# Drawing the order of a weight tile's products and the places of its blocks, tile pair by tile pair

## The chip, the core and the metric

The kernel runs on one core of one Trainium2 chip. The metric is the time of one execution on the device in microseconds (us), taken as the median over runs; smaller is better. A profile is the record of one such execution: each instruction of each engine with its start and its length.

## The reference

Two layers of an encoder over 272 rows (256 tokens and 16 learned rows), model width 2048. In each layer, cut to what matters here:

```
proj = h @ w_in                                # 2048 -> 6176 columns
y    = concat(gated linear attention, neighbourhood attention)
h    = LN(ALPHA * h + y @ w_out)               # 2048 -> 2048
h    = LN(ALPHA * h + relu(h @ w_ff1)**2 @ w_ff2)   # 2048 -> 8192 -> 2048
```

Nearly all arithmetic is in the products with `w_in`, `w_out`, `w_ff1` and `w_ff2`, in float32. After the second layer only the 256 tokens are kept, so much of that layer is computed for 256 columns and not for 272.

## The kernel before, in words

**Two halves for one float32.** TensorE is fed float32r operands. Each weight tile and each activation tile is therefore split into a high part (a rounded copy) and a low part (what the rounding left). A product is the sum of three: weight high by activation high (`h`), weight high by activation low (`l`) and weight low by activation high (`w`).

**A weight tile.** Weights come from HBM in tiles `raw` of 128 partitions by 1024 columns (512 KB), which hold eight blocks of 128 by 128. `made` (L179) takes one tile of the stream, has SP issue its DMA, and `halves` (L208) lets ScalarE copy it to `wh` (L211) and then VectorE subtract `wh` from `raw` into `wl` (L212). There are three buffers of each (`wst`, bufs=3), and `weights` (L173) keeps two tiles made ahead of the one in use. ScalarE can write a `wh` buffer only when the last product that reads it is done, and VectorE a `wl` buffer likewise; the next DMA into a `raw` buffer waits for that subtraction. The engines take their instructions in order.

**Where the blocks lie.** `blocks` makes of a flat tile a triple (access, step, pair): block j starts at `first + j // 2 * pair + j % 2 * step` elements. Before the change `wh` is packed (0, P, 2P): each block starts at a multiple of 512 bytes. For `wl` the constant LOWS gives the places: (16, P+32, 2P+64) where the tile is used in the form called once, and (0, P+48, 2P+64) otherwise. Taken within 256 bytes, the even and the odd low blocks start 64 and 192 bytes in (once), or 0 and 192 bytes in. The activations: the high half starts at a multiple of 256 bytes and the low half at 128 bytes past one (PITCH 288), or directly behind 256 high columns where the pair is dense.

**The products of one tile.** `eight` (L232 to L246) issues all products of a tile in the order of the constant TURNS, with one weight load (PEld) per product (PE):

- not once: "hlhlwwhlhlwwhlhlwwhlhlww", 24 products of 256 to 274 columns each.
- once (second layer, 256 columns, 292 tiles): "hhhhhhhhwwwwwwww". Here the high and low activations stand side by side, and an `h` is one product of 512 columns (high and low activation at once); a `w` has 256. 16 products for a tile.

Four tiles at the end of the last product are loaded for once and used in the other form (`slim`). `by_k` (L256 to L273) uses the weight blocks in an order of its own, with one product per (block, output), and not TURNS. `by_m` calls `eight` for one output block at a time and then lets other work, held in generators, issue some instructions (`pump`): attention, normalisation, evictions.

**What sets the order around the change.** The stream of tiles (`order`) is fixed, tile t+2 is made when tile t is taken, and everything on TensorE is issued in program order.

Of the kernel before, what the change touches and what calls it, by code (L numbers as in the profile page):

```python
# [8 lines left out]
F32R = mybir.dt.float32r  # L9
# [5 lines left out]
P = 128  # L15
# [11 lines left out]
WB = 1024  # L27
# [10 lines left out]
MEET = 2  # L38
PAD = 40
PITCH = 288  # L40
WIDE = 1280
LOWS = {True: (16, P + 32, 2 * P + 64), False: (0, P + 48, 2 * P + 64)}
TURNS = {True: "hhhhhhhhwwwwwwww", False: "hlhlwwhlhlwwhlhlwwhlhlww"}


class Pair(tuple):
# [10 lines left out]
class Trunk:  # L57
    def __init__(self, ctx, tc, ins, out):
        self.ctx, self.tc, self.nc = ctx, tc, tc.nc
        self.i, self.out = ins, out  # L60
        self.bg, self.fg, self.credit, self.fcredit = deque(), deque(), 0, 0
        self.wants, self.due, self.late = {}, None, 0
        self.x = [None] * DC
        self.stream, self.ready = self.order(), deque()
        pool = lambda name, **k: ctx.enter_context(tc.tile_pool(name=name, **k))
        self.cp = pool("const", bufs=1)
        self.xp = pool("xhl", bufs=1)
        self.yp = pool("yhl", bufs=1)
        self.wp = pool("wst", bufs=3)
        self.jp = pool("jn", bufs=1)  # L70
        self.pm = pool("pm", bufs=4, space=PSUM)
        self.pb = pool("pb", bufs=4, space=PSUM)
# [101 lines left out]
    def weights(self):  # L174

        while len(self.ready) < 2:
            self.ready.append(self.made(*next(self.stream, (None, (), False))))
        return self.ready.popleft()

    def made(self, ap, ends, once):  # L180
        if ap is None:
            return None
        nc = self.nc
        raw = self.wp.tile([P, WB], F32, name="raw", tag="raw")
        wh, wl = self.wp.tile([P, WB], F32R, name="wh", tag="wh"), self.wp.tile([P, WIDE], F32R, name="wl", tag="wl")
        wh, wl = self.blocks(wh, 0, P, 2 * P), self.blocks(wl, *LOWS[once])
        for c in map(slice, (0,) + ends, ends):
            nc.sync.dma_start(raw[:, c], ap[:, c])
            self.halves(raw[:, c], wh, wl, slice(c.start // P, c.stop // P))
        if not ends:  # L190
            self.head(ap, raw, wh, wl)
        return wh, wl

    def blocks(self, flat, first, step, pair):

        ap = lambda at, n: bass.AP(flat.tensor, flat.offset + first + at, [flat.ap[0]] + n + [[1, P]])
        return ap, step, pair
# [16 lines left out]
    def head(self, ap, raw, wh, wl):  # L214

        nc, q = self.nc, WB // 4
        both = self.xr.tile([P, 2, q + L], F32, name="head", tag="head", bufs=1)
        self.x[:2] = [self.pair(self.xp, "x", c) for c in range(2)]
        for c in range(2):
            nc.sync.dma_start(both[:, c], self.i["head"][:, c])  # L220
        nc.sync.dma_start(raw[:, 2 * q:], ap[:, 2 * q:])
        for c in range(2):
            at = slice(2 * c, 2 * c + 2)
            h, lo = (t[:, :L] for t in self.x[c])
            acts = lambda: self.split(both[:, c, q:], h, lo)
            weights = lambda: self.halves(both[:, c, :q], wh, wl, at)
            for f in (weights, acts) if c else (acts, weights):
                f()
        for at in (slice(4, 6), slice(6, 8)):
            self.halves(raw[:, at.start * P:at.stop * P], wh, wl, at)  # L230

    def eight(self, ps, wh, wl, x, n, first, last, once):  # L232

        mm = self.nc.tensor.matmul
        seen = dict.fromkeys("hlw", 0)
        for i, kind in enumerate(TURNS[once]):
            j = seen[kind]  # L240
            seen[kind] += 1
            w, v, o = wl if kind == "w" else wh, x[j], ps[:, :n]
            rhs = v[kind == "l"][:, :n]
            if once:
                rhs, o = (v.once, ps) if kind == "h" else (v[0][:, :T], ps[:, T:])
            mm(o, lhsT=self.block(w, j), rhs=rhs, start=first and not i, stop=last and i == len(TURNS[once]) - 1)  # L246

    def whole(self, parts):

# [956 lines left out]
```

## Time and profile before

| | |
|---|---|
| median of 2 runs | 2359.82 us (2359.66 to 2359.98) |
| the profiled execution | 2360.16 us, its span 2358.4 us |
| granted TensorE clock | 0.999 |
| PE, weight loads, VectorE, ScalarE busy | 2348.3, 2234.0, 1523.6, 1213.4 us |
| DMA | 419.02 MB, mean 178 GB/s |
| chain that ended last | PE 97% of the span |

How to read it: PE is the stream of matrix products and PEld that of the weight loads, which run beside them. A row of the groups names line, engine, operation, output tile and input tiles, sizes and count, then the busy time and the mean length of one instruction in ns. Products overlap at their ends, so the length of one is more than its distance to the next one; the distance is read from the starts in the timeline. 16096 of the 18180 products use weight tiles.

### The profile page before, as it was taken

The page shows a single profiled execution, that of the slowest core. Times are in us where ns is not written, and L with a number is a line of the kernel's source. Part 1 is how long each engine was busy: PE and PEld are TensorE (multiplying, and loading weights), DVE is VectorE, ACT ScalarE, POOL GpSimd, SP SyncE. Part 2 cuts the span into 40 slices and gives each one's busy share as a digit, 9 for nine tenths or more (in the row PEclk, how much of TensorE's full clock was granted, in tenths as well). Part 3 has the DMA queues.
Part 4 walks back from the last instruction along what each step waited for, and adds up shares of the span by engine and source line. Part 5 has one row for each costly group of instructions (what it writes and reads, how often), then busy time and mean ns, then how long its engine had stood idle before and what let it go on. Part 6 is the DMA issues. An engine that isn't in the chain of part 4 may idle for free.

```text
span 2358.4 us, 44599 instructions
## 1 busy us (share of the span) xinstructions
PE 2348.3 (100%) x18180; PEld 2234.0 (95%) x18180; DVE 1523.6 (65%) x2432; ACT 1213.4 (51%) x2100; POOL 131.4 (6%) x200
## 2 busy tenths in 40 slices
PE   9999999999999999999999999999999999999998
PEld 9999999999999999999999999999988888888888
DVE  5588777775544455546567787778866545666655
ACT  5666664564433344444457666655654333444443
POOL 0021110110000000000020111100100000000000
PEclk9999999999999999999999999999999999999999
DMA  8454445555555555555555555456566666666664
GB/s 260 153 160 153 151 141 171 170 178 179 176 174 177 177 174 178 178 175 176 177 184 160 174 167 154 156 159 199 182 194 191 193 189 194 189 192 211 202 192 146
DMA packets 118301, 419.02 MB, mean 178 GB/s; under 512 B 13512, under 2 KB 14024, under 8 KB 118096
## 3 DMA queue, kind: packets, MB, share of 16 engines
q1 hardware_dynamic: 117808, 415.65, 56.4%
q8 instruction: 142, 2.33, 0.4%
q10 hardware_dynamic: 288, 0.52, 0.1%
q14 instruction: 63, 0.52, 0.1%
HBM read 414.03 MB, written 2.10 MB: 176 GB/s over the span
## 4 chain that ended last, share of the span: by engine, by line
PE 97%; DVE 2%; issue 1%; ACT 1%; POOL 0%; DVEq 0%; ACTq 0%; POOLq 0%
PE mm L246 85%; PE mm L272 6%; PE bg L272 1%; PE bg L783 1%; PE mm L722 1%; PE bg L583 0%; DVE wl L212 0%; PE bg L429 0%; PE mm L748 0%; DVE acc L1011 0%; ACT wh L211 0%; PE mm L472 0%; PE bg L909 0%; PE bg L634 0%; PE bg L664 0%
## 5 line engine op out<-in xcount | busy, mean ns | idle before, releaser
L212 DVE TENSOR_TENSOR wl<-raw,wh 128x1024 fp32r<-128x1024 f32 (+1 forms) x770 | 942.6, 1225 | 649.1 <-ACT wh L211 644.6
L211 ACT CAST wh<-raw 128x1024 fp32r<-128x1024 f32 (+1 forms) x770 | 805.1, 1047 | 926.8 <-PE mm L246 579.5
L246 PE MATMUL mm<-x,wh 128*128 128x272 f32 (+3 forms) x5376 | 990.5, 311 | 0.0
L246 PEld LDWEIGHTS mm<-x,wh 128*128 128x128 f32 x5376 | 798.4, 188 | 38.6 <-PE mm L722 0.6
L246 PE MATMUL mm<-x,wl 128*128 128x272 f32 (+3 forms) x3264 | 590.1, 284 | 0.0
L246 PEld LDWEIGHTS mm<-x,wl 128*128 128x128 f32 x3264 | 485.4, 188 | 11.4
L246 PE MATMUL mm<-y,wh 128*128 128x272 f32 (+2 forms) x2128 | 411.4, 322 | 0.0
L246 PEld LDWEIGHTS mm<-y,wh 128*128 128x128 f32 x2128 | 325.4, 188 | 22.0
L246 PE MATMUL mm<-u,wh 128*128 128x272 f32 (+2 forms) x1552 | 299.1, 321 | 0.0
L246 PEld LDWEIGHTS mm<-u,wh 128*128 128x128 f32 x1552 | 237.1, 188 | 16.0
L246 PE MATMUL mm<-y,wl 128*128 128x272 f32 (+1 forms) x1408 | 240.5, 282 | 0.0
L246 PEld LDWEIGHTS mm<-y,wl 128*128 128x128 f32 x1408 | 204.3, 188 | 6.4
L246 PE MATMUL mm<-u,wl 128*128 128x272 f32 (+1 forms) x1024 | 175.2, 282 | 0.0
L246 PEld LDWEIGHTS mm<-u,wl 128*128 128x128 f32 x1024 | 148.8, 188 | 4.7
L272 PE MATMUL mm<-x,wh 128*128 128x272 f32 (+1 forms) x512 | 73.5, 289 | 0.0
L272 PEld LDWEIGHTS mm<-x,wh 128*128 128x128 f32 x512 | 67.9, 191 | 0.0
L999 POOL TENSOR_SCALAR acc<-acc,vec 128x272 f32<-128x272 f32 (+1 forms) x24 | 41.9, 1751 | 273.9 <-DVE acc L1011 154.2
L871 DVE TENSOR_TENSOR acc<-acc,mm 128x256 f32<-128x256 f32 (+1 forms) x71 | 30.1, 424 | 38.9 <-PE mm L246 38.9
L560 ACT COPY U<-S 128x272 f32<-128x272 f32 (+1 forms) x104 | 41.0, 429 | 19.3 <-DVE S L569 18.3
L569 DVE TENSOR_TENSOR S<-S,dec 128x272 f32<-128x272 f32 (+1 forms) x112 | 46.1, 441 | 3.7 <-ACT U L560 3.1
L294 ACT CAST u<-ft 128x272 fp32r<-128x272 f32 (+1 forms) x64 | 26.1, 408 | 41.7 <-DVE ft L827 41.7
L571 POOL TENSOR_TENSOR dec<-dec 128x272 f32<-128x272 f32 (+6 forms) x56 | 29.9, 534 | 245.9 <-DVE S L569 245.9
(265 smaller groups left out, 1634.4 us busy)
## 6 DMA issues: line engine op xcount, KB each, us to landing
raw<-in_wff SPq DMA_DIRECT2D x512, 512.0 KB, 3.6
raw<-in_win SPq DMA_DIRECT2D x190, 512.0 KB, 3.9
raw<-in_wout SPq DMA_DIRECT2D x64, 512.0 KB, 3.6
nb<-in_nab SPq DMA_DIRECT2D x16, 352.0 KB, 4.1
xraw<-in_xT SPq DMA_DIRECT2D x7, 272.0 KB, 5.5
out<-out SPq DMA_DIRECT2D x5, 256.0 KB, 3.2
brow<-in_norm SPq DMA_DIRECT2D x4, 256.0 KB, 4.9
gw<-in_wup SPq DMA_DIRECT2D x4, 196.0 KB
```

The costliest lines, as they stand in the source:

```text
L211: self.nc.scalar.copy(h, r)
L212: self.wl = self.nc.vector.tensor_tensor(lo, r, h.bitcast(F32), ALU.subtract).ins
L246: mm(o, lhsT=self.block(w, j), rhs=rhs, start=first and not i, stop=last and i == len(TURNS[once]) - 1)
L272: self.nc.tensor.matmul(ps[g + m][:, :n], lhsT=self.block(parts[p][0], 4 * j + m), rhs=acts[k + j][parts[p][1]][:, :n], start=k + j + p == ...
L294: self.nc.scalar.copy(hi, src)
L560: nc.scalar.copy(U[:, lv % 4, j, :w].rearrange("p (n t h) -> p n t h", t=2, h=hb), bass.AP(S.tensor, S.offset + 2 * j * L, [S.ap[0], [2 * ...
L569: tt(o, o, totals(lv, odd, w), ALU.mult)
L571: nc.gpsimd.tensor_tensor(d[1], d[1], d[0], ALU.mult)
L722: nc.tensor.matmul(ps[hh][:, t * NKEY:t * NKEY + NKEY], lhsT=q[hs, NM + t * P:NM + t * P + P], rhs=k[hs, t, :], start=True, stop=True)
L783: nc.tensor.matmul(po[t][hs, :P], lhsT=v2[ts, hs] if rest else v1[:, t, hs], rhs=p2[ts, hh, :] if rest else p1[:, 2 * hh + t, :], start=re ...
L871: tt(a, a, part, ALU.add)
L999: nc.gpsimd.tensor_scalar(a, a, gain, bias, ALU.mult, ALU.add)
```

## The change

Four things change in the code.

- `wh` gets the size of `wl`, and both are 1344 elements wide (before 1024 and 1280).
- For each tile, `draw` takes a number r from a multiplicative hash of `tiles // 2`, so that two tiles in a row share it. For once it leaves `wh` packed, starts the low blocks 0 to 224 bytes in, in steps of 32 bytes, and puts the odd low block another 0 to 224 bytes on. Otherwise the odd high block, the low tile's start and the odd low block each get 0, 64, 128 or 192 bytes.
- r also picks one of two orders: "hwhw..." or "hhww..." for once, and the former "hlhlww..." or "hllhww..." otherwise.
- A queue `turns` carries the order from the making of a tile to its use; `eight` reads `self.turn`, and falls back to the former order where a tile made for once is used in the other form.

```diff
-WIDE = 1280
-LOWS = {True: (16, P + 32, 2 * P + 64), False: (0, P + 48, 2 * P + 64)}
-TURNS = {True: "hhhhhhhhwwwwwwww", False: "hlhlwwhlhlwwhlhlwwhlhlww"}
+WIDE = 1344
+TURNS = {True: ("hwhwhwhwhwhwhwhw", "hhwwhhwwhhwwhhww"), False: ("hlhlwwhlhlwwhlhlwwhlhlww", "hllhwwhllhwwhllhwwhllhww")}
...
+        self.turn = self.turns.popleft()
         return self.ready.popleft()
...
-        wh, wl = self.wp.tile([P, WB], F32R, name="wh", tag="wh"), self.wp.tile([P, WIDE], F32R, name="wl", tag="wl")
-        wh, wl = self.blocks(wh, 0, P, 2 * P), self.blocks(wl, *LOWS[once])
+        high, low, turn = self.draw(once)
+        wh, wl = self.wp.tile([P, WIDE], F32R, name="wh", tag="wh"), self.wp.tile([P, WIDE], F32R, name="wl", tag="wl")
+        wh, wl = self.blocks(wh, *high), self.blocks(wl, *low)
...
+        self.turns.append(turn)
         return wh, wl
+
+    def draw(self, once):
+
+        r = self.tiles // 2 * 2654435761 % 2 ** 32 >> 8
+        self.tiles += 1
+        if once:
+            return (0, P, 2 * P), (r % 8 * 8, P + r // 8 % 8 * 8, 2 * P + 64), TURNS[once][r // 64 % 2]
+        high, low, base = (r // k % 4 * 16 for k in (1, 4, 16))
+        return (0, P + high, 2 * P + 64), (base, P + low, 2 * P + 64), TURNS[once][r // 64 % 2]
...
-        for i, kind in enumerate(TURNS[once]):
+        turn = self.turn if once or "l" in self.turn else TURNS[False][0]
+        for i, kind in enumerate(turn):
...
-            mm(o, lhsT=self.block(w, j), rhs=rhs, start=first and not i, stop=last and i == len(TURNS[once]) - 1)
+            mm(o, lhsT=self.block(w, j), rhs=rhs, start=first and not i, stop=last and i == len(turn) - 1)
```

More of the change, by code (lines that the diff above doesn't have):

```diff
@@ L63, in __init__ @@
         self.x = [None] * DC
-        self.stream, self.ready = self.order(), deque()
+        self.stream, self.ready, self.tiles, self.turns = self.order(), deque(), 0, deque()
         pool = lambda name, **k: ctx.enter_context(tc.tile_pool(name=name, **k))
@@ L181, in made @@
         if ap is None:
+            self.turns.append(None)
             return None
```

## The prediction

> **What bounds the kernel now.** I read the page first, its busy times and its chain of work.
>
> ```profile
> span 2358.4 us, 44599 instructions
> PE 2348.3 (100%) x18180; PEld 2234.0 (95%) x18180; DVE 1523.6 (65%) x2432; ACT 1213.4 (51%) x2100; POOL 131.4 (6%) x200
> PE 97%; DVE 2%; issue 1%; ACT 1%; POOL 0%; DVEq 0%; ACTq 0%; POOLq 0%
> ```
>
> TensorE never stops: 2348.3 of 2358.4 us. The profiled execution took 2360.16 us, 1.8 us around its span, and stands 0.34 us over the median of 2359.82. So the change matters by two things only: the distance from one weight product to the next, and products that would have to wait for a weight tile. Waits of this kind hardly exist now; the list of waits has one:
>
> ```profile
> PE mm L272 <- DVE wl L212: 0.6, 1, 0.6
> ```
>
> Then the timeline, two tiles of the once form and a stretch of the other form (start, length in us, engine, line).
>
> ```profile
> 2000.33 2.00 PE L246 MATMUL mm<-x,wh 128*128 128x512 f32 x8
> 2002.17 1.08 PE L246 MATMUL mm<-x,wl 128*128 128x256 f32 x8
> 2003.09 2.00 PE L246 MATMUL mm<-x,wh 128*128 128x512 f32 x8
> 2004.93 1.08 PE L246 MATMUL mm<-x,wl 128*128 128x256 f32 x8
> ...
> 699.75 0.41 PE L246 MATMUL mm<-y,wl 128*128 128x272 f32 x2
> ...
> 700.50 0.41 PE L246 MATMUL mm<-y,wl 128*128 128x272 f32 x2
> ```
>
> Take starts, not lengths. Eight `h` of 512 columns take 2004.93 - 2003.09 = 1.84 us, 230 ns each; eight `w` of 256 take 2003.09 - 2002.17 = 0.92, 115 each; a tile 2003.09 - 2000.33 = 2.76. In the other form six products take 0.75 us, 125 ns each, 3.0 us for a tile. Of the groups by shape I now take the mean length (the first number after the comma):
>
> ```profile
> L246 PE MATMUL mm<-x,wh 128*128 128x272 f32 x3584 | 595.4, 288 | 0.0
> L246 PE MATMUL mm<-x,wl 128*128 128x272 f32 x1792 | 367.5, 286 | 0.0
> L246 PE MATMUL mm<-x,wh 128*128 128x512 f32 x1152 | 289.8, 394 | 0.0
> L246 PE MATMUL mm<-x,wl 128*128 128x256 f32 x1152 | 156.6, 278 | 0.0
> L246 PE MATMUL mm<-x,wh 128*128 128x274 f32 x384 | 63.9, 289 | 0.0
> L246 PE MATMUL mm<-x,wl 128*128 128x274 f32 x192 | 40.1, 291 | 0.0
> L246 PE MATMUL mm<-x,wh 128*128 128x258 f32 x256 | 41.5, 285 | 0.0
> L246 PE MATMUL mm<-x,wl 128*128 128x258 f32 x128 | 25.9, 284 | 0.0
> L246 PE MATMUL mm<-u,wh 128*128 128x256 f32 x32 | 5.1, 282 | 0.0
> L272 PE MATMUL mm<-x,wh 128*128 128x256 f32 x128 | 17.6, 283 | 0.0
> L272 PE MATMUL mm<-x,wl 128*128 128x256 f32 x64 | 9.8, 281 | 0.0
> ```
>
> 394 - 230 = 164, 278 - 115 = 163, 288 - 125 = 163: the length is the distance and a constant 163 ns. So a difference of lengths is a difference of distances, and the lengths show what the places do. At 256 columns, packed blocks (all 0 within 256 bytes) have 282 and 283; blocks at 0 and 192 have 281; the `w` of once, at 64 and 192, have 278. That is 4 to 5 ns for not starting where the activation starts. At 272 columns the low blocks (half at 0, half at 192) are only 2 ns shorter than the packed high ones, at 258 one ns, and at 274 they are 2 ns longer.
>
> **The change, part by part.** Counts first. The once form has 292 tiles (2336 products of 512, as many of 256, 4672 in all). The other form has (14752 - 4672) / 24 = 420 tiles, and the by-k form 56.
>
> *High blocks outside once.* Two thirds of 11424 products read a high block, half of them an odd one, 3808; by the formula of the draw 356 of 472 such tiles leave place 0, so some 2871 products start elsewhere. The price for one: the low rows are half off place 0, so the difference of low to high, doubled, is -4 ns (272), -2 (258), -4 (256, by k) and +4 (274). Ends -4 and +4, -11.5 and +11.5 us. I take -1.5, because three of four rows are negative, but the row of 288 mixes products by the high and the low activation, of which the latter (at 128 bytes) never shared a place with a packed block: -4.3 us.
>
> *Low blocks outside once.* Half of 3808 products start at 0 now, a quarter after it: some 936 leave. By the same prices -3.7 to +3.7, taken -1.4 us.
>
> *Low blocks of once.* These stand well now (278). Drawn in steps of 32 bytes, an eighth of 2336 lands on 0 and pays 282 - 277.5 = 4.5 ns: 292 x 4.5 = 1.3 us. If the steps to either side pay the same, it is 35% by the draw, 3.7 us. If other places are better by 1 ns, -2.3. I take +2.5. The high blocks of once stay packed.
>
> A rule that speaks against all three: the Trainium skill, "SBUF — State Buffer", section "Who interferes with whom", gives TensorE two independent read ports, one for the moving operand and one for weight loads, and says that it never waits on anyone. By it these three terms would be 0. The rows of 278 and 282 at one width speak against it as far as TensorE's two reads of itself go.
>
> *The order in once.* What does a change between `h` and `w` cost? Rows for single products of the tile at 2003.09, in this order: the first `h`, then last `h` and first `w` together, then the last three `w`.
>
> ```profile
> L246 PE MATMUL mm<-x,wh 128*128 128x512 f32 x1 | 0.4, 395 | 0.0
> ...
> L246 PE MATMUL mm<-x,wh 128*128 128x512 f32 x1 | 0.4, 389 | 0.0
> L246 PE MATMUL mm<-x,wl 128*128 128x256 f32 x1 | 0.3, 279 | 0.0
> ...
> L246 PE MATMUL mm<-x,wl 128*128 128x256 f32 x3 | 0.5, 276 | 0.0
> ...
> L246 PE MATMUL mm<-x,wh 128*128 128x512 f32 x9 | 2.4, 393 | 0.0
> L246 PE MATMUL mm<-x,wl 128*128 128x256 f32 x10 | 1.5, 277 | 0.0
> ```
>
> An `h` before a `w` is 4 ns shorter than the mean (389 against 393); an `h` behind a `w` is 2 longer and a `w` behind an `h` is 2 longer. "hwhw" has 7 more changes of each sort, "hhww" 3 more; the draw gives 142 and 154 tiles (4 of the 296 are used in the other form). The first sort alone: 142 x -28 ns and 150 x -12 ns, -5.8 us; the other two alone +5.8. After the change each `h` in "hwhw" is of both sorts, so they cancel: 0. The new order "hllhww" outside once changes neither counts nor the last use of a buffer: 0, and any effect lies within the ends above.
>
> *The buffers.* In "hwhw" the last `h` is the last but one product, so ScalarE may overwrite `wh` some 0.8 us later (0.92 less one `w`), and `wl` is needed 230 ns into the tile, not 1.84 us.
>
> ```profile
> 1999.62 1.05 ACT L211 CAST wh<-raw 128x1024 fp32r<-128x1024 f32 x1 [1.44 <-PE mm L246]
> ...
> 2000.58 0.40 ACT L294 CAST y<-ft 128x256 fp32r<-128x256 f32 x1
> 2000.70 1.23 DVE L212 TENSOR_TENSOR wl<-raw,wh 128x1024 fp32r<-128x1024 f32 x1 [0.74 <-ACT wh L211]
> ...
> 2005.84 0.40 PE L246 MATMUL mm<-x,wh 128*128 128x512 f32 x1
> ```
>
> The cast starts when the tile before 2000.33 has done its `h`, so it fills that tile's buffer for the tile that starts at 2005.84. After the change the subtraction would end at 2001.93 + 0.8 = 2002.7 and be needed at 2006.07: 3.3 us are left. What queues behind the waiting cast on ScalarE (a copy of 0.40 us) and on SP (the next `raw`, issued when the subtraction is done) shifts by the same 0.8 us and keeps that slack. The cast's output in blocks: the subtraction already writes such blocks in 1.23 us, and 1.05 + 1.23 on two engines lies beside 2.76 of products; 0. The one thin place is after 1583, where DMAs arrive late:
>
> ```profile
> 1593.88 1.22 DVE L212 TENSOR_TENSOR wl<-raw,wh 128x1024 fp32r<-128x1024 f32 x1
> ...
> 1594.59 2.00 PE L246 MATMUL mm<-y,wh 128*128 128x512 f32 x8
> 1596.43 1.08 PE L246 MATMUL mm<-y,wl 128*128 128x256 f32 x8
> ```
>
> The subtraction ends at 1595.10; `w` starts at 1596.43 and would start at 1594.82, 0.28 us too early. Once TensorE is that much later the tiles behind it fit: +0.5 us, at most 2, at least 0.
>
> Sum: -4.3 - 1.4 + 2.5 + 0 + 0.5 = -2.7. Against its own 2360.16 this gives 2357.5, and 0.34 less for the median: **2357 us**. All low ends: -11.5 - 3.7 - 2.3 - 5.8 = -23.3, 2336.5; all high ends: 11.5 + 3.7 + 3.7 + 5.8 + 2 = 26.7, 2386.5.
>
> **The rivals.**
>
> *Places do nothing* (20%): then only the 0.5 us is left, 2360. For it: 286 and 288 are near. Against it: 278 and 282.
>
> *Places are good everywhere* (10%): 5 ns, as at 256 columns, for the 3807 products that leave place 0, -19, and -5.8 for the order: 2335.
>
> *Places are worse than the chosen ones* (14%): the row of 291 (274 columns) is then the rule, and 3807 x 4 ns + 3.7 + 5.8 + 2 make about +26: 2385.
>
> *A weight load lies open at each change from `w` to `h`* (5%), on the other side. The load of the next `h` has only a short `w` to hide behind.
>
> ```profile
> L246 PEld LDWEIGHTS mm<-x,wl 128*128 128x128 f32 x3264 | 485.4, 188 | 11.4
> 2001.95 1.10 PEld L246 LDWEIGHTS mm<-x,wl 128*128 128x128 f32 x8
> ```
>
> A load is 188 ns long and a `w` stands 115 from the next, so 73 ns could lie open. 142 x 7 + 150 x 3 = 1444 further changes x 73 ns = 105 us: 2465. It decides from 33 ns a change on (47 us). Against it: eight loads in a row take 1.10 us, so loads overlap each other at `w` distance today, and the change that exists, at 2003.09, shows an `h` only 2 ns longer.
>
> *The whole excess goes* (4%). From 256 to 512 columns a product grows by (394 - 278) / 256 = 0.453 ns a column. From the best `w` (276 - 163 = 113) 272 columns would take 120.5, against 125 now: 11424 x -4.5 = -51, and 2336 x -4 for `h` at 389: -61, 2299. Against it: no row at 272 shows it, and the packed high blocks of once are not moved. The Trainium skill, "TensorE: Matmul & The Clock Gate", section "Back-to-back issue gap", states N / 2.4 + 2.5 ns, by which 272 columns would need 116 ns; no row here is that short, and the sum above does not use it.
>
> **How the numbers follow.** My forecast has 47%, with its own range of 2345 to 2370; then 20, 10, 14, 5 and 4%. About 2% (47 us) is what a measurement is taken to tell from no change. Within it lie the forecast and the first three rivals, 91%; slower 5%; faster 4%. The range 2337 to 2387 is that of the ends; it leaves out the last two rivals and most of the second, under 2 in 10.
>
> **What would show it.** Lengths by shape: 272 columns at 286 to 288 (places mixed) or 283 (good everywhere); `w` of once at 278 to 280; `h` of 512 at 392 to 394. An open load would show `h` near 465 in "hwhw" tiles. TensorE should have no new wait longer than 0.5 us, and that one after 1583 on `wl`. I am wrong if lengths at 272 columns move by more than 4 ns, or if waits on `wl` or `wh` appear elsewhere.

## The result, and the profile after

The changed kernel takes 2379.63 us (median of 2 runs, 2379.45 to 2379.81) against 2359.82; the ratio is 1.0085 with a 95% interval of 1.0068 to 1.0102. It is slower, by 19.8 us, where 2.8 us of gain was forecast. The page of the profile after, its span, busy times and chain:

```profile
span 2378.0 us, 44604 instructions
PE 2368.2 (100%) x18180; PEld 2247.8 (95%) x18180; DVE 1528.4 (64%) x2432; ACT 1213.6 (51%) x2100; POOL 127.8 (5%) x200
...
PE 97%; DVE 2%; ACT 1%; issue 0%; POOL 0%; DVEq 0%; ACTq 0%; POOLq 0%
```

TensorE is as busy as before, with the same number of products, and 19.9 us longer: the products themselves stand further apart. No new wait of any size is in the list of TensorE's waits (what was waited for, us in total, times, longest):

```profile
PE mm L285 <- DVE wl L224: 0.4, 1, 0.4
PE mm L259 <- DVE wl L224: 0.2, 1, 0.2
```

The groups by shape (the mean length of one is the number after the comma; line 246 has become 259):

```profile
L259 PE MATMUL mm<-x,wh 128*128 128x272 f32 x3584 | 597.3, 289 | 0.1
L259 PE MATMUL mm<-x,wh 128*128 128x512 f32 x1152 | 383.9, 396 | 0.0
L259 PE MATMUL mm<-x,wl 128*128 128x272 f32 x1792 | 370.5, 288 | 0.3 <-DVE wl L224 0.2
L259 PE MATMUL mm<-x,wl 128*128 128x256 f32 x1152 | 275.7, 280 | 0.0
...
L259 PE MATMUL mm<-x,wh 128*128 128x274 f32 x384 | 64.5, 290 | 0.0
...
L259 PE MATMUL mm<-x,wh 128*128 128x258 f32 x256 | 41.3, 283 | 0.0
```

Of the lengths shown for before, `h` of 512 columns went from 394 to 396, `w` of 256 from 278 to 280, 272 columns from 288 and 286 to 289 and 288; the few of 258 and the `w` of 274 became 1 or 2 ns shorter. (The busy times of these groups are not to be compared: where two groups alternate, the overlapping ends are counted in both.) The timeline of a once tile in the order hwhw:

```profile
2010.54 0.39 PE L259 MATMUL mm<-x,wh 128*128 128x512 f32 x1
2010.77 0.28 PE L259 MATMUL mm<-x,wl 128*128 128x256 f32 x1
...
2013.34 0.40 PE L259 MATMUL mm<-x,wh 128*128 128x512 f32 x1
```

From 2010.54 to 2013.34 lie eight `h` and eight `w`: 2.80 us, where before 2.76 stood. From the starts of all products, each counted up to the next one on TensorE, the tiles of the once form took 808.2 us before and 820.4 after, +12.2; the products of 272 columns that `eight` issues took 1128.6 and 1135.9, +7.3. The other weight products (256, 258 and 274 columns, by-k) stay as they were in sum, and all remaining products add 0.1. Together that is the 19.6 us by which the span grew: the loss is in the weight products of these two forms, and in nothing between them.

The distances by position in the once tile, medians in ns, show what happened:

```
before        h 233 235 229 232 231 226 227 226   w 118 115 115 113 113 113 114 113
after, hwhw   h 232, w 117 throughout
after, hhww   h 233 232, w 118 118 throughout
```

Before, a run starts at 233 and 118 and settles after about five products of `h` at 227 and three of `w` at 113. After, nothing settles: every product stands close to what the first of a run takes.

### The profile page after: what moved, and what is told of

Same layout as the page of the kernel before. It is cut to its first block, busy times and chain, and to the rows that moved or that the text cites. A ratio compares the mean times of both kernels' runs of the same rounds, so it can differ in the third digit from the quotient of the medians.

```text
span 2378.0 us, 44604 instructions
## 1 busy us (share of the span) xinstructions
PE 2368.2 (100%) x18180; PEld 2247.8 (95%) x18180; DVE 1528.4 (64%) x2432; ACT 1213.6 (51%) x2100; POOL 127.8 (5%) x200
## 4 chain that ended last, share of the span: by engine, by line
PE 97%; DVE 2%; ACT 1%; issue 0%; POOL 0%; DVEq 0%; ACTq 0%; POOLq 0%
PE mm L259 85%; PE mm L285 6%; PE bg L285 1%; PE bg L796 1%; DVE wl L224 1%; PE mm L735 1%; PE bg L596 0%; PE bg L442 0%; ACT wh L223 0%; PE mm L761 0%; DVE acc L1024 0%; PE bg L922 0%; PE bg L647 0%; PE mm L485 0%; PE bg L677 0%
## 5 line engine op out<-in xcount | busy, mean ns | idle before, releaser
L259 PE MATMUL mm<-x,wh 128*128 128x272 f32 (+3 forms) x5376 | 1086.9, 311 | 0.1
L259 PE MATMUL mm<-x,wl 128*128 128x272 f32 (+3 forms) x3264 | 712.0, 285 | 0.3 <-DVE wl L224 0.2
L259 PEld LDWEIGHTS mm<-x,wl 128*128 128x128 f32 x3264 | 547.8, 188 | 26.4 <-DVE wl L224 0.6
L259 PE MATMUL mm<-y,wh 128*128 128x272 f32 (+2 forms) x2128 | 465.6, 322 | 0.0
L259 PE MATMUL mm<-u,wh 128*128 128x272 f32 (+2 forms) x1552 | 340.5, 322 | 0.0
L259 PEld LDWEIGHTS mm<-y,wh 128*128 128x128 f32 x2128 | 318.2, 188 | 12.0
L259 PE MATMUL mm<-y,wl 128*128 128x272 f32 (+1 forms) x1408 | 307.6, 284 | 0.0
L259 PEld LDWEIGHTS mm<-y,wl 128*128 128x128 f32 x1408 | 241.9, 188 | 18.3
L259 PEld LDWEIGHTS mm<-u,wh 128*128 128x128 f32 x1552 | 233.6, 188 | 11.2
L259 PE MATMUL mm<-u,wl 128*128 128x272 f32 (+1 forms) x1024 | 228.2, 284 | 0.0
L259 PEld LDWEIGHTS mm<-u,wl 128*128 128x128 f32 x1024 | 176.0, 188 | 10.6
L573 ACT COPY U<-S 128x272 f32<-128x272 f32 (+1 forms) x104 | 40.5, 429 | 19.9 <-DVE S L582 19.2
```

The source lines that it names most:

```text
L573: nc.scalar.copy(U[:, lv % 4, j, :w].rearrange("p (n t h) -> p n t h", t=2, h=hb), bass.AP(S.tensor, S.offset + 2 * j * L, [S.ap[0], [2 * ...
```

## The experiments

Theory A was formed from that table: a product's distance depends on how the addresses of the weight loads and of the moving operand follow each other; a regular run can settle, and a change between `h` and `w` starts it anew. For the first run it was taken narrowly: only those changes cost, and the places do not. Theory B is what my forecast used: a block that starts at the place of the activation costs, one that starts elsewhere does not.

**The places alone.**

```diff
-TURNS = {True: ("hwhwhwhwhwhwhwhw", "hhwwhhwwhhwwhhww"), False: ("hlhlwwhlhlwwhlhlwwhlhlww", "hllhwwhllhwwhllhwwhllhww")}
+TURNS = {True: ("hhhhhhhhwwwwwwww",) * 2, False: ("hlhlwwhlhlwwhlhlwwhlhlww",) * 2}
```

> The drawn places of the change with the two orders of before (eight h then eight w for once, hlhlww otherwise). Theory A, that a tile of the once form pays for each change between h and w: that form stays at 2.75 us a tile, and only the other form's 9 ns a tile (as seen in the changed kernel where it kept hlhlww, 3005 against 2996) is left, 384 tiles, about +4 us: 2363 to 2366. Theory B, that the low blocks at 64 and 192 bytes were the best places and the draw loses them: the once form goes to 2.80 us, 292 x 47 ns = 13.6 us, in all +18: 2377.

2374.68 us, ratio 1.0064 (1.0051 to 1.0076): +14.7. That refutes A in its narrow form (2363 to 2366) and is nearer to B's 2377, though not for B's reason, as the scans below show. From here on A stands in the wide form: the places decide too. The once form takes 817.0 us (+8.8), the 272 columns 1134.4 (+5.8). In the by-shape groups the `h` of 512 columns keep their 394 and the `w` go from 278 to 281:

```profile
L259 PE MATMUL mm<-x,wl 128*128 128x272 f32 x1792 | 370.1, 288 | 0.0
L259 PE MATMUL mm<-x,wh 128*128 128x512 f32 x1152 | 290.3, 394 | 0.0
...
L259 PE MATMUL mm<-x,wl 128*128 128x256 f32 x1152 | 159.7, 281 | 0.0
```

The timeline shows it in the runs: eight `h` still 1.84 us (2012.29 - 10.45), eight `w` 0.95 (2013.24 - 12.29) in place of 0.92.

```profile
2010.45 2.00 PE L259 MATMUL mm<-x,wh 128*128 128x512 f32 x8
2012.29 1.11 PE L259 MATMUL mm<-x,wl 128*128 128x256 f32 x8
2013.24 2.00 PE L259 MATMUL mm<-x,wh 128*128 128x512 f32 x8
```

With drawn places a run of `w` stays at 118 from the first to the last. By the rule of the Trainium skill, "SBUF — State Buffer", section "Who interferes with whom", that TensorE has two independent read ports and never waits on anyone, this kernel should equal the one before. The 14.7 us say otherwise, as far as TensorE's own two reads go.

**The order alone.**

```diff
-            return (0, P, 2 * P), (r % 8 * 8, P + r // 8 % 8 * 8, 2 * P + 64), TURNS[once][r // 64 % 2]
+            return (0, P, 2 * P), (16, P + 32, 2 * P + 64), TURNS[once][r // 64 % 2]
...
-        return (0, P + high, 2 * P + 64), (base, P + low, 2 * P + 64), TURNS[once][r // 64 % 2]
+        return (0, P, 2 * P), (0, P + 48, 2 * P + 64), TURNS[once][r // 64 % 2]
```

> The drawn orders of the change with all blocks at the places of before. Theory A (changes between h and w cost): once tiles at 2.80 us, +13.6 us, and half of the other tiles in hllhww, at most 8 ns each: 2374 to 2376. Theory B (places cost): once tiles stay at 2.75 us, 2360 to 2362.

2378.68 us, ratio 1.0081 (1.0067 to 1.0095): +18.7, a little more than A's 2374 to 2376, and B's 2360 to 2362 is refuted as a whole account. The once form takes 820.6 us (+12.4): the median tile 2827 ns in hwhw and 2782 in hhww, where 2754 stood. At 272 columns the median tile in the old order keeps 2997 ns and in hllhww takes 3014; +6.3 us in all.

```profile
L259 PE MATMUL mm<-x,wh 128*128 128x512 f32 x1152 | 384.5, 396 | 0.0
L259 PE MATMUL mm<-x,wl 128*128 128x272 f32 x1792 | 369.0, 287 | 0.2 <-DVE wl L224 0.2
L259 PE MATMUL mm<-x,wl 128*128 128x256 f32 x1152 | 275.6, 280 | 0.0
```

So each half of the change costs nearly the whole, 14.7 and 18.7, and both together 19.8. In once the halves cost 8.8 and 12.4 and both 12.2, at 272 columns 5.8 and 6.3 and both 7.3. In once they do not add up because they spoil the same thing, the settled runs: once they are gone, the other half finds little to spoil. That the buffers of this kernel are also larger costs nothing: the tiles in the old order keep their 2997 ns, and a kernel below with the old buffers has the same 2827 ns in hwhw.

**Runs of four and of sixteen.**

```diff
-TURNS = {True: "hhhhhhhhwwwwwwww", False: "hlhlwwhlhlwwhlhlwwhlhlww"}
+TURNS = {True: "hhhhwwwwhhhhwwww", False: "hlhlwwhlhlwwhlhlwwhlhlww"}
```

> The kernel before with hhhhwwwwhhhhwwww for once, nothing else changed. Theory A in the form that the distance settles along a run (233, 235, 229, 232, 231, 226, 227, 226 for h and 118, 115, 115, 113 and so on for w in the kernel before): a tile takes twice the first four of each, 2 x (929 + 461) = 2780 ns, +27 ns x 292 = +7.8 us: 2367 to 2368. If instead each alternation cost a fixed sum, two more changes of each sort at (2800 - 2753) / 7 = 6.7 ns per pair, which only hwhw has 7 of and hhww 3 of though both take 2800: 2362. Theory B: no change, 2360.

2365.50 us, ratio 1.0026 (1.0016 to 1.0036): +5.5, a tile 2773 ns; A's form that settles said 2780 and +7.8, a fixed sum per change +2, B nothing. The time lies between the first two and nearer to settling. The distances are 232 236 228 229 and 118 116 114 113, the first four of a long run but for the last `h`.

```diff
-        for i, kind in enumerate(TURNS[once]):
+        for i, kind in enumerate(TURNS[once][::-1] if once and self.odd else TURNS[once]):
...
+                self.odd = k // 8 % 2
                 self.eight(ps, wh, wl, acts[k:k + 8], n, not k, k == nk - 8, once)
```

> The kernel before, but every second tile of an output block in the once form issues its eight w first and then its eight h, so that runs of sixteen w and sixteen h arise across tile borders. Theory A, settling: the half of the tiles that go on with a settled run save what the first products of each kind pay above the last, about 26 ns for h and 10 ns for w, so half of 36 ns on 292 tiles each: -5 us, 2354 to 2356. Theory B: no change. Against a gain: the low tile of every second weight tile is needed at its start, 1.8 us earlier, which may cost up to 2 us where the subtractions are late.

2355.64 us, ratio 0.9982 (0.9973 to 0.9991): 4.3 us faster than the kernel before, as A said, and the best version of this study. The timeline has the long runs, and a few products out of it, by narrow windows, show how they settle: four of the first `h` of the run at 2003.14 (394 in the mean), six later ones (389), then two early `w` of the run at 2006.80 (278) and seven later ones (276).

```profile
2003.14 3.81 PE L246 MATMUL mm<-x,wh 128*128 128x512 f32 x16
2006.80 1.99 PE L246 MATMUL mm<-x,wl 128*128 128x256 f32 x16
2008.62 3.14 PE L246 MATMUL mm<-x,wh 128*128 128x512 f32 x13
```

```profile
L246 PE MATMUL mm<-x,wh 128*128 128x512 f32 x4 | 1.1, 394 | 0.0
...
L246 PE MATMUL mm<-x,wh 128*128 128x512 f32 x6 | 1.5, 389 | 0.0
...
L246 PE MATMUL mm<-x,wl 128*128 128x256 f32 x2 | 0.4, 278 | 0.0
...
L246 PE MATMUL mm<-x,wl 128*128 128x256 f32 x7 | 1.0, 276 | 0.0
```

Sixteen `h` take 3.66 us, 229 each, sixteen `w` 1.82, 114 each. In the medians of the tiles after 1569 us the second half of a run stands at 227 and 113 in nearly every product, though it reads another weight tile than the first half, and where an output block ends (50 runs of `h` on `x`) also goes back to the first activation.

**Which places settle.** Two scans put the blocks of each pair of tiles at one of 64 settings from a list, with the orders of before; each kernel ran once. After 1570 us each setting has two to four tiles of once, and these are read tile by tile.

```diff
+        p = self.seen[once] // 2
+        self.seen[once] += 1
+        at, step = p % 16 * 4, P + (32, 0, 16, 48)[p // 16 % 4]
+        return (0, P, 2 * P), (at, step, 2 * P + 64)
```

> The kernel before, its orders kept, with the low blocks of each pair of tiles at places of a list in place of the fixed ones: the start in steps of 16 bytes from 0 to 240, the odd block 128, 0, 64 or 192 bytes further within 256 (640, 512, 576 or 704 bytes behind the even one). Only the distances of the products tile by tile are read. Theory A (the places of before are one special point for w): only the start at 64 bytes with 640 between blocks shows w at 113 to 114 ns in a run, nearly all others 117 to 120. Theory B (what counts is not to share the place of the activation): all starts except 0 and its neighbours show 113 to 114. In the other form theory A expects tiles between 2985 and 3040 ns with no order by the place alone.

Of the 64 settings of the low blocks, just one lets a run of `w` settle below 115 ns in the tiles after 1570 us: a start at 64 bytes with 640 between blocks, the setting of before. (The 40 once tiles ahead of that, whose activation halves lie 1152 bytes apart and not side by side, do not settle in the kernel before either: 2808 ns.) Two of the four tiles that have it stand in the timeline between others, whose start is 16 bytes lower or higher:

```profile
1913.85 1.11 PE L254 MATMUL mm<-u,wl 128*128 128x256 f32 x8
1914.79 2.01 PE L254 MATMUL mm<-y,wh 128*128 128x512 f32 x8
1916.64 1.08 PE L254 MATMUL mm<-y,wl 128*128 128x256 f32 x8
1917.55 2.00 PE L254 MATMUL mm<-y,wh 128*128 128x512 f32 x8
1919.39 1.08 PE L254 MATMUL mm<-y,wl 128*128 128x256 f32 x8
1920.31 2.01 PE L254 MATMUL mm<-u,wh 128*128 128x512 f32 x8
1922.15 1.11 PE L254 MATMUL mm<-u,wl 128*128 128x256 f32 x8
1923.10 0.63 PE L254 MATMUL mm<-u,wh 128*128 128x512 f32 x2
```

Eight `w` take 0.91 and 0.92 us in the two, 0.94 and 0.95 in their neighbours. Theory B is refuted: starts far from 0 are no better than 0. The kernel takes 2376.00 us. Not every run starts high, either. With the low blocks packed like the high ones (start 0, 512 bytes on), the first `w` stands 113 ns from the next and the last six 120. The mean lengths of the first and of three later ones:

```profile
L254 PE MATMUL mm<-y,wl 128*128 128x256 f32 x1 | 0.3, 278 | 0.0
...
L254 PE MATMUL mm<-y,wl 128*128 128x256 f32 x3 | 0.5, 283 | 0.0
```

```diff
+        return (at, step, 2 * P + 64), LOWS[once]
```

> The same list of places for the high blocks (low ones as before). Theory A: the eight h start at about 232 wherever the blocks lie, and some places may let them settle sooner than after five products (227) or not at all; tiles of once 2720 to 2800. Theory B: packed blocks at 0 share the activation's place and are the worst, so most places give 226 from the first h on, 2725 a tile.

With the low blocks held at the good setting, 22 of the 64 settings of the high ones let the `w` settle (113 to 114 ns, same tiles) in every tile, 14 more in one tile of each pair and not in the other, and 28 in neither. So whether a run of `w` settles depends on the run of `h` ahead of it too. The packed blocks at 0, by B the worst, share the second place of 64 (2753 ns a tile, the best 2749, the last 2829). In the best one (start 64 bytes, 704 between blocks) `h` never settles: it repeats 227, 225, 236, 232 to the end of the run, and the `w` behind it stand at 113 from the first. So the rise at the start of a run belongs to the places of before and is no general price of a first product. 2374.17 us.

**One other place for all tiles.**

```diff
-LOWS = {True: (16, P + 32, 2 * P + 64), False: (0, P + 48, 2 * P + 64)}
+LOWS = {True: (0, P + 32, 2 * P + 64), False: (0, P + 48, 2 * P + 64)}
```

> The kernel before with the low blocks of once at 0 and 640 bytes in place of 64 and 704, the same for all tiles, order as before. If the place itself counts (theory A), w stays at 117 to 120 and the tile at about 2.79 us, +10 us: 2370. If only the drawing counts, since tiles then follow each other without order, a place that is held gives 2753 ns a tile and 2360.

2368.64 us, ratio 1.0040 (1.0028 to 1.0053), +9.2: the `w` stay at 116 to 120, their length at 281, the median tile at 2813 ns, and the once form takes 817.6 us (+9.4). So a place that is held for all tiles costs as much as the drawn ones: it is not the drawing that costs, but that the places are not the ones of before.

```profile
L246 PE MATMUL mm<-x,wl 128*128 128x256 f32 x1152 | 159.3, 281 | 0.0
```

**What a change between `h` and `w` changes.** It changes the half of the PSUM bank, the width and the weight tile. First the half, in the order hwhw for all tiles:

```diff
-                rhs, o = (v.once, ps) if kind == "h" else (v[0][:, :T], ps[:, T:])
+                rhs, o = (v.once, ps) if kind == "h" else (v[0][:, :T], ps[:, :T])
```

> The kernel before with hwhwhwhwhwhwhwhw for once and each w added into the lower half of the PSUM bank in place of the upper (the halves are summed later either way). If the jump of the output to the other half is what unsettles the distances, tiles return to 2.75 us and the time to 2360. If not, they stay at 2827 ns as with this order at fixed places, 292 x 74 ns = +21.6: 2381.

2378.79 us; `h` 235 and 236, `w` 117 and 118, the very values of hwhw with the upper half, where 2381 was expected without an effect of the half and 2360 with one. The PSUM half plays no part.

```profile
L246 PE MATMUL mm<-x,wh 128*128 128x512 f32 x1152 | 407.8, 398 | 0.0
...
L246 PE MATMUL mm<-x,wl 128*128 128x256 f32 x1152 | 323.3, 281 | 0.0
```

Then one width for both:

```diff
-                rhs, o = (v.once, ps) if kind == "h" else (v[0][:, :T], ps[:, T:])
+                rhs, o = v.once, ps
```

> The kernel before with each w taken over all 512 columns (weight low by activation low is added, more than the reference needs), so that h and w have one width, one moving operand and one output. If the change of width is what unsettles the distances, all sixteen products stand at 226 to 228. If the change of the weight tile does it, the first h of a tile again stand at 232 to 236. The time rises by 292 x 8 x 113 ns = 264 us to about 2624 in either case.

2628.12 us. The `h` behind a run of `w` still start high and settle, 236 228 233 231 227 227 227 226, although width, moving operand and output are now the same on both sides. Single products of the run at 2204.00, the first and a later group:

```profile
L246 PE MATMUL mm<-x,wh 128*128 128x512 f32 x1 | 0.4, 397 | 0.0
...
L246 PE MATMUL mm<-x,wh 128*128 128x512 f32 x5 | 1.3, 390 | 0.0
```

What is left is the move from the low blocks to the high ones; the activation also goes back from the eighth to the first. The runs of sixteen show that another weight tile and that step back do not start a run anew by themselves: their ninth product has both and stays at 227. So the other places of the blocks are what remains, by exclusion. The `w` at this width do not settle at all (226 to 237), at the places where they settle at 256 columns.

**Runs outside once.** Three kernels tried to carry the finding over to the 272-column products: eight `h`, eight `l`, eight `w`; the same with every second tile reversed; the same with the low blocks at the places of once.

```diff
-TURNS = {True: "hhhhhhhhwwwwwwww", False: "hlhlwwhlhlwwhlhlwwhlhlww"}
+TURNS = {True: "hhhhhhhhwwwwwwww", False: "hhhhhhhhllllllllwwwwwwww"}
```

> The kernel before with eight h, eight l and eight w in a row outside once; all have one width there. If any regular run settles, as the runs of once do, the tiles fall from 2996 by some ns a product, 385 x 24 x 2 to 4 ns = 18 to 37 us: 2323 to 2342. If settling also needs the right places, the sign is open: 2350 to 2375.

```diff
-        for i, kind in enumerate(TURNS[once]):
+        for i, kind in enumerate(TURNS[once][::-1] if self.odd else TURNS[once]):
```

> As the last, and every second tile of an output block in both forms issues its products in reverse order, so that runs go on across tile borders. The once form saves the 4.3 us of the runs of sixteen; outside once the gain over the kernel with runs alone is half of what the first products of a run pay: 4 to 9 us if runs settle there, nothing if not.

```diff
-LOWS = {True: (16, P + 32, 2 * P + 64), False: (0, P + 48, 2 * P + 64)}
+LOWS = {True: (16, P + 32, 2 * P + 64), False: (16, P + 32, 2 * P + 64)}
```

> Runs of eight outside once, and the low blocks there at the places of once (64 bytes, then 640 on). If that place settles a run of w by itself, w outside once falls below 121 ns; if the special point belongs to 256 columns and dense activations only, w stays at 123 to 126 and the time within 5 us of that with runs alone.

They take 2366.26 (ratio 1.0031, 1.0019 to 1.0042), 2368.20 (1.0036, 1.0024 to 1.0049) and 2368.47 us (1.0039, 1.0025 to 1.0052). None has the hoped-for gain: in the first the distances at 272 columns run from 122 to 130 without settling, and the median tile takes 3007 ns against 2997. In the second, once saves 4.7 us as in the runs of sixteen, but the 272 columns lose 11.2, of which 1.0 is one wait for `wl`. A run by itself is not enough. Lengths of the first kernel:

```profile
L246 PE MATMUL mm<-x,wh 128*128 128x272 f32 x3584 | 488.7, 289 | 0.0
...
L246 PE MATMUL mm<-x,wl 128*128 128x272 f32 x1792 | 260.8, 288 | 0.0
```

A closer spacing exists at 272 columns, though, and the kernel before has it now and then: 28 of its 376 such tiles take 2932 to 2953 ns and not 2997, seven of them in a row from 78 to 98 us. Six products there take 0.73 us (81.70 - 80.97) in place of 0.75, with the same order and the same places as everywhere else:

```profile
80.97 0.65 PE L246 MATMUL mm<-x,wh 128*128 128x272 f32 x4
81.46 0.41 PE L246 MATMUL mm<-x,wl 128*128 128x272 f32 x2
81.70 0.65 PE L246 MATMUL mm<-x,wh 128*128 128x272 f32 x4
```

So order and places inside a tile do not fix the distance alone; something ahead of the tile or beside it counts too, and no run separates the two. Were all 376 tiles so, 376 x 64 ns = 24 us would be saved, an estimate; no run shows how to get there.

## Why the prediction was wrong

The forecast was a gain of 2.7 us, summed from small terms of both signs. **The order in once** is the step that failed most: taken at 0 with ends of 5.8 us, it cost 12.4 us alone. I had the rows that showed it, first `h` 395 and last 389, but read them as two prices of two kinds of border, behind and ahead of a change, and let them cancel. They were the two ends of one settling: position in the run counts, and an order without runs has only early positions. Comparing the mean of the first four (394) with that of the last four (390) would have shown a slope, where border prices of this size make 1 to 2 ns. Position is not the whole of it: the first distances of a run from the kernel before give 2808 ns for hwhw and 2804 for hhww, and the run with the order alone has 2827 and 2782.

**The low blocks of once**, taken at +2.5 with an end of 3.7 us, cost 8.8. Here theory B failed: I took 278 for the normal state and 282 for the price of place 0. With most places the length is 280 to 281, and 278 was the one setting of 64 that settles.

**The blocks outside once** were taken at -5.7; the places alone cost +5.8 there, inside the end but with the other sign. The 2 ns between the high and low rows at 272 columns were no price of place 0: in the scan of the low places the four settings that start at 0 take 2933, 2943, 2990 and 3015 ns a tile, where all 64 run from 2933 to 3038. The new order hllhww, taken at 0, costs 17 ns in the median tile and 6.3 us in all.

**The buffers**, taken at 0.5 us, cost nothing, but not as worked out. The wait of 0.28 us after 1583 did not come: all tiles of that stretch drew hhww, and the thinnest had 0.84 us left between its subtraction and its first `w`. The one new wait on `wl`, 0.2 us, stands at 1299 us in a tile of 272 columns, which had 0.06 us to spare before. **The open weight load** did not come: `h` stands at 396 in length, not 465.

"Places are worse than the chosen ones" was a rival at 2385 with 14%, and its number is the nearest. That a tuned setting is lost is what the runs show, but it reached its 26 us with 15.2 for the blocks outside once, where 5.8 was measured, and with 5.8 for the order in once, where 12.4 was. That the measured time lies inside the range of 2337 to 2387 is luck: the range adds up all ends, and the order in once and its low blocks each went beyond their own. Of the signs, `w` of once at 280 came out, `h` at 396 lay outside 392 to 394, and lengths at 272 columns moved by 2 ns at most, so that sign would not have told. Two slips in the working weigh little: 138 tiles took hwhw, not 142, and 154 hhww, not 150; and that rival's terms add up to 26.7.

The Trainium skill, "TensorE: Matmul & The Clock Gate", section "Back-to-back issue gap", gives N / 2.4 + 2.5 ns for an isolated product on the warm clock; estimates from it are 109 for 256 and 216 for 512 columns. The settled runs here stand at 113 and 227, and the unsettled ones at 118 and 233, so no run of this case comes down to it.

What stays open: by which mechanism in TensorE the addresses act, why 272-column runs and 512-column `w` runs do not settle at the places tried, why some settings of the high blocks keep the following `w` from settling, and what sets the products of 28 tiles of 272 columns closer together. The runs show that it is so, not why.

## What to carry to other kernels

Where TensorE is 100% busy, read the distances of its products position by position, not as one mean: a slope along a run is time that longer runs may give back, 4.3 us here in once and nothing at 272 columns. A tuned layout may sit on a narrow point, 1 setting of 64 here for the low blocks, so neither a neighbour 16 bytes away nor a mean over many settings tells what it is worth, and spreading over settings gives the mean, which is worse. Two edits that spoil the same state do not add up; test each alone before adding their prices.

## What was not expected of the hardware

The distance between products of 512 columns varies from 226 to 236 ns in the medians, and of 256 columns from 113 to 120, while TensorE waits about 4 us in all before and after alike and the clock stands at 0.999 to 1.0, by the order of the weight tiles and by 16 bytes in where a block starts. At the places of before it takes about five products of a run for `h` and three for `w` to come down; at others the distances rise along a run, or repeat with a period of four.
